# Hyena's transforms ahead of retention's six projections in the program's order

## The chip, the core and the metric

The kernel runs on one core of a Trainium2 chip. The core's engines run side by side, each through its own list of instructions in the order of that list, and they wait for each other at semaphores: TensorE (PE, with its weight loads as PEld), VectorE (DVE), ScalarE (ACT), GpSimd (POOL) and SyncE (SP), which here only issues DMAs. The metric is the device time of one execution in microseconds (us), lower is better.

## The reference

One inference step of a two-layer trunk over 384 token rows: 128 context tokens and 256 latent tokens, model width 1024. Each layer does, with norms and modulation vectors that come from a condition vector:

```
h = rms_norm(x) * (1 + scale1) + shift1
ret, hy, gqa, mla = split(h @ w_in)
y = concat(retention(ret), hyena(hy), attention(gqa), latent_attention(mla)) @ w_out
x = x + gate1 * rms_norm(y)
h = rms_norm(x) * (1 + scale2) + shift2
x = x + gate2 * rms_norm((silu(dwconv3(h @ up_gate)) * (h @ up_val)) @ w_down)
```

The mixers that matter here are two. Hyena takes three slices of 256 channels, convolves them over three neighbours, and then does, for two orders in turn, a long convolution by way of a Fourier transform:

```
z = x1 * ifft(fft(v) * spec0)
y_hy = x2 * ifft(fft(z) * spec1)
```

Retention projects queries, keys and gates, forms decayed scores q.k over 4 heads, sums them with the values and a carried state, normalises by head and multiplies by silu(gate). The context group also returns its retention state.

## The kernel before

All matrix products of the model's width are done in a split form: a weight unit of 512 KB is loaded by a DMA into a tile `raw` (a ring of five, `wraw`, L361), ACT casts it to `whi` (L358), DVE takes the rest as `wlo` (L359), each in two halves, and PE multiplies three times (`mm3`, L382 to L385). One input projection of 128 channels (`fm_mm`, tile `fmps`) is 24 matmuls of 386 columns. The pairs `whi`, `wlo` of the mixers form a ring of three.

In each layer the mixers come in the program's order latent attention, grouped attention (`gqa`), Hyena, retention, output projection. Attention up to its last key projection stands in an order written out by hand; from there to the output projection a scheduler places instructions. It walks through time on a model of the engines, takes on each engine what is ready, and among several the one that stands first in the program. So the program's order is a priority, and what stands behind can fill gaps. Once built, the order on each engine is fixed, and so is the order of the DMAs on SP's queue.

Hyena and retention are generators, each cut in two by a `yield`:

- `hyena` (L1069): the first part is six projections, the short convolution (L1078 to L1080) and transposes to token rows (`hyt`, L1095). The second part is the transforms: for each of two orders, six forward matmuls (`hyR`, `hyI`, `hyQ`, L1102 to L1105), a product with the spectrum `spec` on DVE (`Y`, with a scratch tile `t12`, L1113 to L1117) whose last sum is POOL's (L1118), and the inverse: `hyAB`, `hyP` (L1122 to L1126) and the multiplication by x1 (`hz`, `ut`, L1130 to L1136) in the first order, `hyF` (L1142 to L1146) and the multiplication by x2 in the second.
- `retention` (L1160): the first part is value tables and the six projections (L1180 to L1189), the second is decays, scores (`rpc`, `rsc`), sums (`rob`), norms (`rrb`, L1267) and the result.

A third strand is the modulation vectors. Layer 0 has to compute those of two groups of its own (`Ada`): 16 steps, each of which loads two 512 KB tiles `araw` through the same ring of five and multiplies them (`adaps`, L407). A step is taken from the list `side` by each projection (`fm_proj`) and by each of Hyena's two orders (L1100); `run(side[0])` does what is left. In layer 1 the list has one short step.

`spec` has one buffer. Layer 1's spectrum is loaded into it by a DMA of 1536 KB that is written in the feed-forward part of layer 0 (L1548) and may go once layer 0's Hyena has read the old one for the last time.

Behind the mixers stands the output projection (`acc`, L1283 to L1285), with eight weight units, and its first matmuls are the filler for retention's second part.

Of the kernel before, what the change touches and what calls it, by code (L numbers as in the profile page):

```python
# [268 lines left out]
def trunk(ctx: ExitStack, tc: tile.TileContext, A, O, offs, depth=DEPTH):  # L269
# [79 lines left out]
    def bank(tag="a", name="bk"):  # L349
        kw = {"bufs": 1} if tag == "n" else {}  # L350
        return (pa if tag == "a" else pm).tile([128, 512], F32, tag=tag, name=name, **kw)
# [9 lines left out]
    def wraw(src, n=1024):  # L361
        raw = wr.tile([128, 1024], F32, tag="raw", name="raw")[:, 0:n]
        nc.sync.dma_start(out=raw, in_=src)
        return raw

    def wparts(n=1024, pool=None, bufs=4):
        kw = {"bufs": bufs} if pool is not None else {}
        return [(pool or wh).tile([128, 1024], F32R, tag=g, name="w" + g, **kw)[:, 0:n] for g in ("hi", "lo")]

    def wsplit(raw, hi, lo, h, eng=None):  # L370
        n = raw.shape[1] // 2
        sl = slice(h * n, h * n + n)
        split(raw[:, sl], hi[:, sl], lo[:, sl], eng)
# [89 lines left out]
    def ada(a, out, k1=8, part=False):  # L463

        for k in range(a.k0, k1):
            a.load(k)
            a.mm(k, last=k1 - 1)
            if k < k1 - 1:
                yield
        if part:  # L470
            a.hold(k1)
        else:
            a.load_end()
            a.end()
            a.columns()
            a.vec(out)
        yield

    def ada_last(a, out):
        a.columns()  # L480
        a.vec(out)
        yield
# [41 lines left out]
    def gate_tiles(ggp):  # L524
        return [ggp.tile([128, D], F32, tag="gg", name="gg", bufs=2) for _ in range(2)]
# [5 lines left out]
    def load_lp(l):  # L531
        t = lpp.tile([128, A["lp"].shape[2]], F32, tag="lp", name="lp")
        nc.sync.dma_start(out=t, in_=A["lp"][l])

        def get(name, a=0, b=None):
            o, w = poff[name]
            return t[:, o + a:o + (w if b is None else b)]

        fh = lpp.tile([128, NF, 4], F32, tag="ffh", name="ffh")
        V.tensor_scalar(fh.rearrange("p f t -> p (f t)"), get("ffc"), 0.5, None, ALU.mult)  # L540

        lg = get("lg")
        W = lg.shape[1]
        e = sm.tile([128, W], F32, tag="lge", name="lge", bufs=1)
        s = sm.tile([128, W], F32, tag="lgs", name="lgs", bufs=1)
        s2 = sm.tile([128, W], F32, tag="lgs2", name="lgs2", bufs=1)
        pol = sm.tile([128, W], F32, tag="lgp", name="lgp", bufs=1)
        lgt = lpp.tile([128, W], F32, tag="lgt", name="lgt")
        S.activation(out=e, in_=lg, func=ACTF.Abs)
        S.activation(out=e, in_=e, func=ACTF.Exp, scale=-1.0)  # L550
        V.tensor_scalar(s, e, 2.0, None, ALU.add)
        V.reciprocal(s, s)
        V.tensor_tensor(out=s, in0=e, in1=s, op=ALU.mult)
        V.tensor_tensor(out=s2, in0=s, in1=s, op=ALU.mult)
        V.tensor_scalar(pol, s2, 2.0 / 19, 2.0 / 17, ALU.mult, ALU.add)
        for d in (15, 13, 11, 9, 7, 5, 3, 1):
            V.tensor_tensor(out=pol, in0=pol, in1=s2, op=ALU.mult)
            V.tensor_scalar(pol, pol, 2.0 / d, None, ALU.add)
        V.tensor_tensor(out=pol, in0=pol, in1=s, op=ALU.mult)
        V.scalar_tensor_tensor(out=lgt, in0=lg, scalar=0.0, in1=pol, op0=ALU.min, op1=ALU.subtract)  # L560
        return get, fh, lgt
# [148 lines left out]
    def retention_tables(lgt, pool, **kw):  # L710
        lag = pool.tile([128, 384], F32, name="lag", **kw)
        nc.sync.dma_start(out=lag, in_=A["lag"])
        return rettab(lgt, lambda: pool.tile([128, 384], F32, name="tabt", **kw), lag)
# [111 lines left out]
    def run(g):  # L825
        for _ in g:
            pass
# [538 lines left out]
    for l in range(depth):  # L1366
# [4 lines left out]
        with ExitStack() as ph:  # L1371
            mt = ph.enter_context(tc.tile_pool(name="mt", reuse_waits="tile", bufs=1))
            lmt = mt.tile([128, A["lm"].shape[2]], F32, tag="lm", name="lm")

            def M(name):
                o, w = moff[name]
                return lmt[:, o:o + w]

            mx = ph.enter_context(tc.tile_pool(name="mx", reuse_waits="tile", bufs=1))
            myc = tc.tile_pool(name="my", reuse_waits="tile", bufs=1, side="right")  # L1380
            my = myc.__enter__()

            jobs = [ada_last(ahead.pop((l, 1)), vecs)] if l else [ada(Ada(l, 1), vecs), ada(Ada(l, 2), vecs)]
            side[:] = [(s for j in jobs for s in j), 0]
            tma = mx.tile([128, 3, 416], F32, tag="tma", name="tma")
            tmb = my.tile([128, 3, 384], F32, tag="tmb", name="tmb")
            wa, wb = pj, TokProj(l, "wtb", 384, ht)
            us = []
            ml = mla(l, mx, my, M, tmb, tma, wb.acc)
            gq = gqa(l, mx, my, M, hi, lo, tma, lambda: get("sink"), us)  # L1390
            with tc.manual_schedule(engines=CORE | {mybir.EngineType.SP}):
                wa.raw(3)
                for c in range(4):
                    wb.raw(c)
                wa.cut(3, 0)
                wa.cut(3, 1)
                wa.part(3, (0, 1, 2))
                uw = [wraw(A["win"][l, 2])]
                nc.sync.dma_start(out=lmt, in_=A["lm"][l])
                next(ml)  # L1400
                next(gq)
                if l == 0:
                    nc.sync.dma_start(out=cst, in_=A["cst"])
                wb.cut(0, 0)
                wb.cut(0, 1)
                wa.out(tma)
                wb.part(0, (0, 1, 2))
                uw.append(wraw(A["win"][l, 0]))
                for c in range(1, 4):
                    wb.cut(c, 0)  # L1410
                    wb.cut(c, 1)
                    wb.part(c, (0, 1, 2))
                next(ml)
                us.append(wparts())
                wsplit(uw[0], *us[0], 0)
                wsplit(uw[0], *us[0], 1)
                next(ml)
                next(gq)
                us.append(wparts())
                wsplit(uw[1], *us[0], 0)  # L1420
                wsplit(uw[1], *us[0], 1)
                next(ml)
                next(gq)
                end = V.tensor_copy(zero8, zero8)
            if l == 0:
                mkf = hm.tile([128, 256], F32, tag="hm", name="mkf")
                nc.sync.dma_start(out=mkf, in_=A["mask"])
                with tc.issue_after(end.ins):
                    V.tensor_copy(maskb, mkf)
                    lps = load_lp(0)  # L1430
                    rt = retention_tables(lps[2], mx, tag="w15", bufs=11)
            get, fh, lgt = lps
            run(ml)
            run(gq)
            hyg = hyena(l, mx, my, get, sp, hi, lo)
            reg = retention(l, mx, M, get, rt, hi, lo, tma)
            next(hyg)
            next(reg)
            run(side[0])
            run(hyg)  # L1440
            side[0] = iter(())
            myc.__exit__(None, None, None)
            run(reg)

            wqc = tc.tile_pool(name="wq", reuse_waits="tile", bufs=4, side="right")
            wq = wqc.__enter__()
            gg = gate_tiles(wq)

            b6 = [bank("m" if i < 5 else "n", "acc") for i in range(6)]
            acc = [b6[0:2], [b6[2], b6[5]], b6[3:5]]  # L1450
            with tc.manual_schedule(engines={mybir.EngineType.SP}):
                early = [(wunit(A["wout"][l, k]), mixout[k]) for k in (6, 7, 4)]
                for ts in ((0, 1), (2,)):
                    for j, e in enumerate(early):
                        down_step(acc, *e, T0, j == 0, False, ts)
                ws = [(wunit(A["wout"][l, k]), mixout[k]) for k in (5, 2, 3)]
                ws += [(wunit(A["wout"][l, k], 1024, wq), mixout[k]) for k in (0, 1)]
                up_w = [wunit(A["wup"][l, u], 1024, wq) for u in (0, NF)]
                for r in range(2):
                    gate_load(gg, 2 * (l % 2), r)  # L1460
# [158 lines left out]
```

## Time and profile before

| what | us |
|---|---|
| median of 3 runs | 1088.33 (1086.99 to 1088.36) |
| the profiled execution | 1084.69 |
| its span, first to last instruction | 1082.9 |
| PE busy | 1059.6 (98%) |
| DVE busy | 727.2 (67%) |
| ACT busy | 504.3 (47%) |
| POOL busy | 61.5 (6%) |

PE's busy time includes the run of a matmul through the array, so a full PE row does not mean that each instruction followed the one before at once; the distance from start to start tells that. In layer 0 Hyena's and retention's work of interest lies from 165 to 238 us, in layer 1 from 690 to 758 us.

### The profile page before, as it was taken

To read this page: it belongs to the slowest core of one execution; us is meant where nothing else is said; L and a number is where in the kernel's file an instruction comes from. 1 tells how busy PE (TensorE), PEld (TensorE's weight loads), DVE (VectorE), ACT (ScalarE), POOL (GpSimd) and SP (SyncE) were. 2 spreads that over 40 slices of the span, in tenths; PEclk is the share of its full clock that TensorE was granted. 3 is DMA by queue.
4 is the path that set the end of the run, shared out by engine and by line. 5 is a ranking of instruction groups with operands and counts; after the bars stand their busy time and mean duration, and the time that the engine had idled before them with its cause. 6 is when DMAs were issued, how large, how long until landed. Compare 5 with 4: busy or idle time off the path is not lost.

```text
span 1082.9 us, 15620 instructions
## 1 busy us (share of the span) xinstructions
PE 1059.6 (98%) x5763; PEld 894.1 (83%) x5763; DVE 727.2 (67%) x1544; ACT 504.3 (47%) x1106; POOL 61.5 (6%) x74
## 2 busy tenths in 40 slices
PE   9999999999889999999999999999999999999997
PEld 4496767768789999899996977886899999999996
DVE  5868965476789885799557577757766455545544
ACT  5754635334734344333447454552584344334333
POOL 2210000000200000000002000001020000000000
PEclk9999999999999999999999999999999999999999
DMA  9674345855576764577356522231535433443301
GB/s 345 231 278 169 118 155 178 302 168 222 180 250 201 226 215 150 159 234 221 124 169 209 179 79 77 60 97 41 217 109 191 129 117 118 136 131 122 119 19 58
DMA packets 53017, 176.05 MB, mean 163 GB/s; under 512 B 8618, under 2 KB 10538, under 8 KB 52429
## 3 DMA queue, kind: packets, MB, share of 16 engines
q1 hardware_dynamic: 49229, 171.19, 47.2%
q10 hardware_dynamic: 3712, 3.87, 1.0%
q8 instruction: 45, 0.74, 0.3%
q14 instruction: 31, 0.25, 0.1%
HBM read 169.60 MB, written 5.44 MB: 162 GB/s over the span
## 4 chain that ended last, share of the span: by engine, by line
PE 86%; DVE 8%; DMA 2%; ACT 2%; issue 1%; POOL 0%; ACTq 0%; DVEq 0%; SPq 0%; POOLq 0%
PE ups L383 5%; PE ups L385 5%; PE ups L384 5%; PE gps L383 5%; PE facc L1283 5%; PE facc L1285 5%; PE gps L385 5%; PE gps L384 5%; PE facc L1284 5%; PE fmps L383 4%; PE fmps L385 4%; PE fmps L384 4%; PE adaps L407 2%; PE acc L1283 2%; PE acc L1284 2%; PE acc L1285 2%
## 5 line engine op out<-in xcount | busy, mean ns | idle before, releaser
L359 DVE TENSOR_TENSOR wlo<-raw,whi 128x512 fp32r<-128x512 f32 (+2 forms) x388 | 254.4, 686 | 169.0 <-ACT whi L358 168.5
L358 ACT CAST whi<-raw 128x512 fp32r<-128x512 f32 (+2 forms) x388 | 221.6, 611 | 276.5 <-DMA raw<-in_wdn_dram 99.1
L1283 PE MATMUL facc<-whi,fah 128*128 128x512 f32 x264 | 105.3, 399 | 2.7 <-ACT fah L358 2.7
L1285 PE MATMUL facc<-whi,fal 128*128 128x512 f32 x264 | 104.5, 397 | 0.2 <-DVE fal L359 0.2
L1284 PE MATMUL facc<-wlo,fah 128*128 128x512 f32 x264 | 104.5, 396 | 0.0
L505 DVE SCALAR_TENSOR_TENSOR avc<-avr,cs,avc 128x1024 f32<-128x1024 f32 x56 | 70.3, 1282 | 0.3 <-DMA avr<-in_ada_dram 0.2
L383 PE MATMUL gps<-hTa,whi 128*128 128x386 f32 (+4 forms) x184 | 62.5, 340 | 0.0
L383 PE MATMUL ups<-hTb,whi 128*128 128x386 f32 (+4 forms) x184 | 61.7, 335 | 0.6 <-ACT hTb L812 0.6
L384 PE MATMUL ups<-hTb,whi 128*128 128x386 f32 (+4 forms) x184 | 61.4, 334 | 0.8 <-POOL hTb L815 0.8
L385 PE MATMUL gps<-hTa,wlo 128*128 128x386 f32 (+4 forms) x184 | 62.0, 337 | 0.0
L384 PE MATMUL gps<-hTa,whi 128*128 128x386 f32 (+4 forms) x184 | 61.8, 336 | 0.0
L383 PE MATMUL gps<-hTb,whi 128*128 128x386 f32 (+4 forms) x184 | 61.7, 335 | 0.0
L383 PE MATMUL ups<-hTa,whi 128*128 128x386 f32 (+4 forms) x184 | 61.7, 335 | 0.0
L385 PE MATMUL ups<-hTb,wlo 128*128 128x386 f32 (+4 forms) x184 | 61.5, 334 | 0.0
L385 PE MATMUL gps<-hTb,wlo 128*128 128x386 f32 (+4 forms) x184 | 61.4, 334 | 0.0
L385 PE MATMUL ups<-hTa,wlo 128*128 128x386 f32 (+4 forms) x184 | 61.4, 334 | 0.0
L384 PE MATMUL ups<-hTa,whi 128*128 128x386 f32 (+4 forms) x184 | 61.3, 333 | 0.0
L384 PE MATMUL gps<-hTb,whi 128*128 128x386 f32 (+4 forms) x184 | 61.3, 333 | 0.0
L1285 PEld LDWEIGHTS facc<-whi,fal 128*128 128x128 f32 x264 | 50.0, 189 | 13.1 <-DVE fal L359 1.3
L1283 PEld LDWEIGHTS facc<-whi,fah 128*128 128x128 f32 x264 | 50.0, 189 | 13.0 <-ACT fah L358 3.0
L1284 PEld LDWEIGHTS facc<-wlo,fah 128*128 128x128 f32 x264 | 50.0, 190 | 10.1
L1299 ACT ACTIVATE fth<-fc 128x386 f32<-128x386 f32 x44 | 23.2, 528 | 59.9 <-DVE fc L1298 59.9
(381 smaller groups left out, 2371.4 us busy)
## 6 DMA issues: line engine op xcount, KB each, us to landing
raw<-in_wup_dram SPq DMA_DIRECT2D x88, 512.0 KB
araw<-in_ada_dram SPq DMA_DIRECT2D x64, 512.0 KB
raw<-in_wdn_dram SPq DMA_DIRECT2D x44, 512.0 KB
avr<-in_ada_dram SPq DMA_DIRECT2D x32, 512.0 KB
raw<-in_win_dram SPq DMA_DIRECT2D x30, 512.0 KB
raw<-in_wout_dram SPq DMA_DIRECT2D x16, 512.0 KB
gg<-gd SPq DMA_DIRECT2D x8, 512.0 KB
raw<-in_wta_dram SPq DMA_DIRECT2D x8, 416.0 KB
```

Of the source, the lines that this page charges most:

```text
L358: S.copy(hi, src)
L359: (eng or V).tensor_tensor(out=lo, in0=src, in1=hi, op=ALU.subtract)
L383: T.matmul(out, ah, bh, start=start, stop=False)
L384: T.matmul(out, ah, bl, start=False, stop=False)
L385: T.matmul(out, al, bh, start=False, stop=stop)
L407: T.matmul(self.ps[32 * j:32 * j + 32, :], cs[:, k, :], rows[j // 2][:, 512 * (j % 2):512 * (j % 2) + 512], start=(k == self.k0), stop=(k ...
L505: V.scalar_tensor_tensor(out=acc[:, v, c], in0=raw, scalar=sc, in1=acc[:, v, c], op0=ALU.mult, op1=ALU.add)
L1283: T.matmul(acc[t][h], ah[:, cs_], wh_[:, hs], start=first, stop=False)
L1284: T.matmul(acc[t][h], ah[:, cs_], wl_[:, hs], start=False, stop=False)
L1285: T.matmul(acc[t][h], al[:, cs_], wh_[:, hs], start=False, stop=last)
L1299: S.activation(out=th, in_=c, func=ACTF.Tanh)
```

## The change

```
@@ -1434,10 +1434,10 @@
             run(gq)
             hyg = hyena(l, mx, my, get, sp, hi, lo)
             reg = retention(l, mx, M, get, rt, hi, lo, tma)
-            next(hyg)
+
+            run(hyg)
             next(reg)
             run(side[0])
-            run(hyg)
             side[0] = iter(())
             myc.__exit__(None, None, None)
             run(reg)
```

Before, the program had Hyena's projections, retention's projections, Hyena's transforms, retention's second part. Now it has Hyena's projections, Hyena's transforms, retention's projections, retention's second part. No instruction of the model's arithmetic is added or taken away. In layer 0, the two steps of the list `side` that Hyena's orders ask for now find something to take, so two steps of the modulation vectors move ahead of retention's first projection.

PE in layer 1, before: from the second half of the first order's forward matmuls on.

```order
L1104 MATMUL hyQ<-ut,cst 128x256
L1105 MATMUL hyQ<-ut,cst 128x256
L1204 MATMUL rkt<-cst_79,rf_7091 128x128
L1204 MATMUL rkt<-cst_79,rf_7126 128x128
L1283 MATMUL acc<-whi,mix 128x512
L1284 MATMUL acc<-wlo,mix 128x512
L1285 MATMUL acc<-whi,mix 128x512
L1213 MATMUL rst<-rpack 64x128 x4
L1225 MATMUL rpc<-rf_7021,rf_7091 128x128
L1225 MATMUL rpc<-rf_7056,rf_7126 128x128
L1283 MATMUL acc<-whi,mix 128x512
L1122 MATMUL hyAB<-Y,cst 128x256 x2
```

The same place of layer 1 in the changed kernel, up to the second order's first matmul (`rf` are retention's projected rows, `mix` the mixers' results).

```order
L1104 MATMUL hyQ<-ut,cst 128x256
L1105 MATMUL hyQ<-ut,cst 128x256
L1122 MATMUL hyAB<-Y,cst 128x256 x2
L1124 MATMUL hyAB<-Y,cst 128x256 x2
L1125 MATMUL hyP<-Y,cst 128x256
L1126 MATMUL hyP<-Y,cst 128x256
L1102 MATMUL hyR<-ut,cst 128x256
```

And the end of the second order there, where the projections follow.

```order
L1105 MATMUL hyQ<-ut,cst 128x256
L1142 MATMUL hyF<-cst,Y 128x128 x4
L1144 MATMUL hyF<-cst,Y 128x128 x4
L1145 MATMUL hyF<-cst,Y 128x128 x2
L1146 MATMUL hyF<-cst,Y 128x128 x2
L383 MATMUL fmps<-hTa,whi 128x386
```

Retention's tail no longer stands between Hyena's matmuls; from the first `hyt` to the last `hyF` of layer 1 PE's list has nothing but Hyena, and four of retention's six projections (96 matmuls) follow in one piece. The other two stand ahead of `hyt`, as fillers of grouped attention, before and now.

SP's queue in layer 0, before: from Hyena's last weight unit (`raw_1853`) to retention's second (`raw_1979`); the first is `raw_1927`.

```order
L363 DMA raw_1853<-in_win_dram 128x1024
L399 DMA araw_1900<-in_ada_dram 128x1024
L399 DMA araw_1902<-in_ada_dram 128x1024
L422 DMA abg_1908<-in_adag_dram 128x1024
L363 DMA raw_1927<-in_win_dram 128x1024
L399 DMA araw_1962<-in_ada_dram 128x1024
L399 DMA araw_1964<-in_ada_dram 128x1024
L399 DMA araw_1971<-in_ada_dram 128x1024
L399 DMA araw_1973<-in_ada_dram 128x1024
L363 DMA raw_1979<-in_win_dram 128x1024
```

The same stretch of SP's queue in the changed kernel, up to retention's first weight unit, now `raw_2048`.

```order
L363 DMA raw_1853<-in_win_dram 128x1024
L399 DMA araw_1890<-in_ada_dram 128x1024
L399 DMA araw_1892<-in_ada_dram 128x1024
L422 DMA abg_1898<-in_adag_dram 128x1024
L399 DMA araw_1959<-in_ada_dram 128x1024
L399 DMA araw_1961<-in_ada_dram 128x1024
L399 DMA araw_2040<-in_ada_dram 128x1024
L399 DMA araw_2042<-in_ada_dram 128x1024
L363 DMA raw_2048<-in_win_dram 128x1024
```

Four loads of modulation weights stand ahead of retention's first unit that stood behind it; the unit takes the place that its second unit had, and on PE the first of retention's projections moves from ahead of grouped attention's last softmax to behind eight `adaps` matmuls that follow it.

A second place on the same queue in the changed kernel: layer 1's spectrum, between retention's third unit (`raw_2142`) and its fourth (`raw_2193`).

```order
L363 DMA raw_2142<-in_win_dram 128x1024
L399 DMA araw_2177<-in_ada_dram 128x1024
L399 DMA araw_2179<-in_ada_dram 128x1024
L1548 DMA spec_3535<-sd_96 128x3072
L399 DMA araw_2185<-in_ada_dram 128x1024
L399 DMA araw_2187<-in_ada_dram 128x1024
L363 DMA raw_2193<-in_win_dram 128x1024
```

Before, this DMA stood behind all of retention's units and behind seven of the eight of the output projection.

## Rows read from the trace of the kernel before

**Rows 1.** The page's first part: busy us, share, instructions.

```profile
PE 1059.6 (98%) x5763; PEld 894.1 (83%) x5763; DVE 727.2 (67%) x1544; ACT 504.3 (47%) x1106; POOL 61.5 (6%) x74
```

**Rows 2.** Waits of PE, whole span: us in total, times, longest us.

```profile
PE tps L799 <- DVE xn L792: 4.5, 3, 2.0
PE hyF L1144 <- POOL Y L1118: 1.1, 2, 0.7
```

**Rows 3.** Windows of layer 1: busy PE, PEld, DVE, ACT, POOL, clock, DMA, GB/s.

```profile
730.00:740.00 10.00, 10.00 (x51) 6.83 (x51) 8.62 (x22) 0.74 (x2) 1.99 (x2) 1.00 0.08 13
740.00:750.00 10.00, 9.57 (x68) 6.00 (x69) 8.63 (x25) 1.43 (x4) 2.72 (x4) 1.00 0.18 55
```

**Rows 4.** Timeline of PE, layer 1: start, us, instruction, [idle before].

```profile
722.06 0.34 PE L383 MATMUL fmps<-hTa,whi 128*128 128x386 f32 x1
...
726.32 0.59 PE L1102 MATMUL hyR<-ut,cst 128*128 128x256 f32 x2
...
727.18 0.59 PE L1102 MATMUL hyR<-ut,cst 128*128 128x256 f32 x2
...
737.33 0.59 PE L1102 MATMUL hyR<-ut,cst 128*128 128x256 f32 x2
...
743.45 1.16 PE L1144 MATMUL hyF<-cst,Y 128*128 128x128 f32 x8 [0.43 <-POOL Y L1118]
```

**Rows 5.** Timeline of DVE, layer 1.

```profile
708.17 1.23 DVE L1091 COPY fo<-cv 128x128 f32<-128x128 f32 x2
...
728.33 0.69 DVE L1113 TENSOR_TENSOR Y<-hyR,spec 128x512 f32<-128x512 f32 x1
...
732.79 0.43 DVE L1114 TENSOR_TENSOR t<-hyQ,spec 128x256 f32<-128x256 f32 x1 [0.72 <-POOL Y L1118]
...
736.35 0.42 DVE L1135 TENSOR_TENSOR ut<-hz 128x256 f32<-128x256 f32 x1
...
737.02 1.41 DVE L1242 TENSOR_TENSOR rW<-rsc,tab 128x256 f32<-128x256 f32 x4
738.89 0.69 DVE L1113 TENSOR_TENSOR Y<-hyR,spec 128x512 f32<-128x512 f32 x1 [0.46 <-PE hyR L1102]
```

**Rows 6.** Timeline of POOL, layer 1.

```profile
731.49 1.27 POOL L1118 TENSOR_TENSOR Y<-Y,t 128x512 f32<-128x512 f32 x1 [22.18 <-DVE t L1117]
...
744.93 0.72 POOL L1118 TENSOR_TENSOR Y<-Y,t 128x256 f32<-128x256 f32 x1 [1.54 <-DVE t L1117]
```

**Rows 7.** Timeline of PE, layer 0, end of grouped attention.

```profile
169.06 0.45 PE L383 MATMUL fmps<-hTa,whi 128*128 128x386 f32 x1
...
171.29 0.82 PE L925 MATMUL ptp<-cst,P 128*128 128x128 f32 x6
...
178.64 1.92 PE L407 MATMUL adaps<-araw,cs 128*32 128x512 f32 x16
```

**Rows 8.** Timeline of DVE, layer 0, the last long softmax.

```profile
170.48 1.40 DVE L922 TENSOR_SCALAR P<-P,rc 128x384 f32<-128x384 f32 x4
```

**Rows 9.** Timeline of SP's queue, layer 0: start of issue, us, DMA.

```profile
156.58 0.33 SPq L363 DMA_DIRECT2D raw<-in_win_dram  x1
...
173.53 0.33 SPq L363 DMA_DIRECT2D raw<-in_win_dram  x1
...
227.39 0.33 SPq L1548 DMA_DIRECT2D spec<-sd  x1
```

**Rows 10.** Windows of both layers, columns as in Rows 3.

```profile
792.00:793.00 1.00, 0.00 (x0) 0.00 (x0) 0.96 (x2) 0.83 (x3) 0.91 (x1) 1.00 0.00 0
794.00:797.00 3.00, 3.00 (x16) 3.00 (x15) 1.37 (x4) 1.56 (x5) 0.72 (x2) 0.50 0.02 5
620.00:625.00 5.00, 3.57 (x11) 1.74 (x10) 3.90 (x7) 4.63 (x11) 0.00 (x0) 1.00 0.45 132
210.00:215.00 5.00, 4.90 (x28) 4.14 (x27) 3.71 (x12) 2.15 (x5) 0.73 (x1) 1.00 0.88 313
```

**Rows 11.** DMA issues, whole span: what, count, KB each.

```profile
spec<-sd SPq DMA_DIRECT2D x1, 1536.0 KB
```

More of the change, by code (lines that the diff above doesn't have):

```diff
@@ L1436, in trunk @@
             reg = retention(l, mx, M, get, rt, hi, lo, tma)
-            next(hyg)
+            run(hyg)
             next(reg)
             run(side[0])
-            run(hyg)
             side[0] = iter(())
```

## The prediction

> **What bounds the kernel now.** I read the page's first part, then PE's waits, then windows and timelines of the two stretches in which Hyena and retention lie. PE is busy for 1059.6 of 1082.9 us [rows 1]; there is no second engine near it, and anything that leaves PE without work is added to the time. The waits of PE are few: the longest group, 4.5 us, lies at norms outside the stretches that the change touches, and of Hyena's transforms 1.1 us are on record, for POOL's sum ahead of `hyF` [rows 2]. The reader is to see in the windows of layer 1 that PE is full, or nearly, from 730 to 750 us while DVE works 8.6 of 10 us [rows 3]: two chains, Hyena's transforms and retention's tail, alternate there, and each fills PE while the other waits for DVE. That cover is what the change takes away. So there is next to nothing to win: 0.4 us of idle in layer 1 [rows 3, 4], the other 0.7 us of the `hyF` wait in layer 0, and perhaps 0.6 us where PE changes less often between the transforms and the 512-column matmuls of the output projection.
>
> **Layer 1: the transforms alone on PE.** In the changed order PE has nothing but Hyena from `hyt` to the last `hyF`. I work out how long that chain is by itself, and how much of it is PE's own work.
>
> The chain, first order. From `hyR` to DVE's first product: 737.33 to 738.89, that is 1.56 us [rows 4, 5]. From that product to the new `ut` that the second order needs: 728.33 to 736.35 plus its 0.42 and a hand-over of 0.1, 8.5 us, of which one product of retention (0.33 us) was in DVE's way and goes: 8.2 us [rows 5]. In it lies the wait of DVE for POOL, which holds the only scratch tile for 1.27 us [rows 5, 6]; that stays, since POOL's sums are the same. Sum 9.8 us. Second order: again 1.56 us, then from the product at 738.89 to the end of POOL's second sum at 744.93 + 0.72 [rows 5, 6], 6.8 us, then the last two `hyF`, some 0.6 us: 9.0 us. Both: 18.8 us.
>
> PE's own work in it: 18 matmuls of 256 columns, of which `hyR` and `hyI` take 0.86 us together (726.32 to 727.18), 0.43 us each, 7.7 us; 12 of 128 columns, of which four take 1.1 us (743.45), 0.27 us each, 3.2 us; and some ten restarts at an estimated 0.1 us. That is 11.9 us [rows 4]. So PE stands 18.8 - 11.9 = **6.9 us**. Bounds: 5 us if the hand-overs that I read beside other work are shorter by themselves, 8.5 us if each of some eight hand-overs costs 0.2 us more than in my reading.
>
> Two smaller terms. Ahead of `hyR` the transposes wait for copies of DVE that take 1.23 us from 708.17 [rows 5], beside POOL's products of retention; before, two projection matmuls stood in that wait and now none: **0.5 us** (0 to 1). And retention's tail now has only the output projection between its parts. PE there waits for DVE's four products `rW` (1.41 us at 737.02 [rows 5]) before each of the two sums `rob`, which Hyena's matmuls covered; 0.3 us of `rob` on other inputs and what there is of the output projection take some of it off: 1 us for each, **2.0 us** (1 to 3). Four projections in one piece take 4 x 4.26 us (722.06 to 726.32 for one [rows 4]), as before; their weights have long landed. Less the 0.4 us and the 0.6 us named above, layer 1 costs 0.5 + 6.9 + 2.0 - 1.0 = **8.4 us**.
>
> **Layer 0: the weights come later.** Here the transforms do have fillers: nine to eleven projection matmuls and a few `adaps` in each gap. Going through the same chain with them between, I find gaps of 0.8 us in all (0 to 4, the upper end if the fillers' weights are late): **0.8 us**. The costs come from SP's queue.
>
> First, retention's first unit is issued behind four more loads of modulation weights. It waits for a ring buffer that comes free late, as its second unit did before: at 173.53 instead of 156.58 [rows 9]. Its 24 matmuls, 4.3 us of PE, began at 169.06 and ran inside grouped attention's last softmax [rows 7]. Without them PE stands from 169.06 until the first normalised scores, which DVE begins at 170.48 [rows 8]: 1.85 us; and 0.9 us more in the waits between `ptp` at 171.29 and the scores before 178.64, where five of the 24 stood. The rest of the 24 covered nothing and is merely done later. **2.8 us** (1.5 to 4.3, all of it).
>
> Second, layer 1's spectrum. Its DMA was issued at 227.39 [rows 9], behind all of retention's weights; now it stands ahead of retention's fourth unit and blocks the queue until Hyena's last read of the old spectrum. Layer 0's first `hyR` I put near 185.5: the eight `adaps` of 178.64 [rows 7] start 1.4 us earlier without projections ahead of them and end at 179.2, and 14 projection matmuls (2.5 us), the short softmax and `hyt` (3.8 us, an estimate) follow. The last read is about 19 us behind it, by the chain above with fillers in its gaps: 204.7. Then 1536 KB of spectrum, two `araw` and the unit itself, 512 KB each, must come in [rows 11], 3 MB in all, at the 313 GB/s that the stretch from 210 to 215 us showed [rows 10]: 10 us, so the unit lands near 214.5, and cast and remainder take 1 us more. PE has 1.8 us of `adaps` behind the chain's end near 206.5, one projection (4.3 us) and 1 us of `adaps`, and is there at 213.6. **2.0 us** for this unit, **0.7 us** for the next one, which queues behind it (together 0 to 6: nothing if the chain is through earlier or the spectrum shares the DMA engines gently, 6 if the unit lands last of all that is queued). DVE and ACT are not in the way there: they wait for the same weights. Third, retention's tail as in layer 1, with a little more filler: **1.5 us** (0.5 to 3). Less 0.7 us of old waits, layer 0 costs 2.8 + 0.8 + 2.7 + 1.5 - 0.7 = **7.1 us**.
>
> **The sum.** 8.4 + 7.1 = 15.5 us. The profiled execution took 1084.69 us with a span of 1082.9, so its changed counterpart would take 1100.2. The three timed runs have their median 3.64 us above the profiled execution, at 1088.33, and the forecast goes by them: 1103.8, **1104 us**. Behind the mixers everything is bound to PE's own order, so nothing absorbs the delay; the feed-forward parts are moved as a whole.
>
> **Rivals.**
> *PE's clock falls in the new gaps.* In layer 1's norms PE's longest wait is 2.0 us [rows 2]; from 792 to 793 it had nothing at all, with the granted clock still at 1.00, and from 794 to 797 it worked all the while with the clock at 0.50, its lower level of 1.2 GHz [rows 10]. Three us at half speed cost 1.5 us. Against it: from 620 to 625 PE was busy only 3.57 of 5 us, in shorter pauses, and the clock stayed at 1.00 [rows 10]. The new gaps of layer 1 are 0.6 to 1.5 us each by the chain above, seven in a row; the one at 169.06 in layer 0 is 1.85 us. If four of them bring a fall, it is 6 us more, 1110 us.
> [...]
>
> *Only layer 1 pays.* If layer 0's weights are in time after all, because PE, held up, also asks later, and the grouped attention finds its cover in `adaps`, layer 0 costs nothing: 1088.3 + 8.4 = 1097 us. For it: PE was busy for 4.90 of 5 us where the DMA engines were fullest before [rows 10], so weights were in time. Against it: the missing 24 matmuls at 169.06 are in the order, whatever lands when.
>
> *The two chains gain by being apart* (the other side). DVE is at 8.6 of 10 us where they run together [rows 3]. If that made each of them slow, so that PE's full row there hides weight loads and drains rather than work, then retention's tail by itself, with a free DVE and Hyena's results long there for the output projection, would run through it without a wait, and the transforms would cost only the difference. It decides from the point at which retention's tails are shorter than before by more than all the terms above, 15.5 + 1.7 us in two layers. If the tail by itself took as much off as the transforms add, and 1.7 us of old waits were won beside, the time would be 1088.3 - 1.7 = 1087 us. I see no row for it beyond DVE's share; the idle on record leaves it only those 1.7 us and what PE's restarts hide.
>
> **How the numbers follow.** The forecast has 0.60, the clock 0.20, layer 1 alone 0.15, the gain 0.05. The terms' own bounds make 5 to 11 us of layer 1 and 1.5 to 13 of layer 0, not all at one end at once. For 8 in 10 I take 1095 to 1113 us: it holds the forecast's middle, layer 1 alone, and most of the clock's case. 0.2%, some 2 us, is what a measurement of this kernel can tell from none. Slower by more than that is all of the first three cases, 0.94 with a remnant of the fourth taken off; the fourth is split between no change, 0.04, and faster, 0.02.
>
> **What would show it.** In layer 1, PE's timeline between the first `hyR` and the first projection behind the last `hyF` should be about 19 us long, with idle of 6 to 7 us put down to DVE's `Y`, POOL's `Y` and ACT's `hbs`; PE's wait list should have `hyAB`, `hyP`, `hyR` and `hyF` in it, where now only `hyF` is. Retention's `rob` should wait for `rW`. In layer 0, PE should stand for near 2 us ahead of `ptp` at about 169 us, and a projection should wait for ACT's `whi` or DVE's `wlo` at about 214 us, with the spectrum's DMA issued near 205. The forecast is wrong if PE is as full in 726 to 750 us as before, or if the gaps are there and the out-projection behind them has become shorter by as much.

## The result, and the profile after

The changed kernel took 1103.64 us (median of 4 runs, 1100.11 to 1108.62) against 1087.66 us for the kernel before in the runs beside it: a ratio of 1.0155, 95% interval 1.0111 to 1.0199. It is slower, and the forecast of 1104 us holds to 0.4 us. A second set of runs of the same kernel gave 1106.45 us and 1.0186 (1.0167 to 1.0206). What follows shows that the total was met with sizes and causes that were partly others than those of the working.

The profiled execution took 1103.06 us, with a span of 1101.3. The page's first part answers to [rows 1]:

```profile
PE 1067.1 (97%) x5763; PEld 895.4 (81%) x5763; DVE 729.1 (66%) x1544; ACT 504.5 (46%) x1106; POOL 62.6 (6%) x74
```

PE has the same 5763 instructions and stands 34.2 us instead of 23.3. But it is also 7.5 us longer *busy* with them. So a list of waits tells only part of the loss.

PE's waits over the whole span, as in [rows 2] (us in total, times, longest):

```profile
PE ptp L925 <- DVE P L922: 2.7, 2, 1.9
...
PE fmps L383 <- ACT rf L1182: 1.4, 1, 1.4
PE hyAB L1122 <- DVE Y L1115: 1.4, 1, 1.4
PE hyF L1144 <- POOL Y L1118: 1.2, 2, 0.8
...
PE hyR L1102 <- DVE ut L1135: 0.9, 1, 0.9
...
PE fmps L383 <- ACT whi L358: 0.9, 1, 0.9
PE hyAB L1124 <- POOL Y L1118: 0.8, 1, 0.8
...
PE fmps L385 <- DVE wlo L359: 0.8, 1, 0.8
...
PE hyP L1126 <- POOL Y L1118: 0.4, 1, 0.4
PE rob L1260 <- ACT rsq L1258: 0.4, 1, 0.4
```

The waits that were named are there, but for one: `ptp` in layer 0's softmax, the four kinds at Hyena's transforms in layer 1 (for DVE and POOL, none for ACT's `hbs`), `whi` and `wlo` in layer 0. Retention's `rob` does not wait for `rW`, but 0.4 us for ACT's `rsq`. One was not named: 1.4 us ahead of a projection, for ACT's copy `rf`.

Where the time lies is read stage by stage. The rows of the transposes `tps` mark each norm in PE's timeline; the table has the time from the start of the last such row in one norm to that in the next, in us, for all kernels of this study. "Rest" runs from layer 1's second norm to PE's last matmul:

| profiled run | layer 0 mixers | layer 0 feed-forward | layer 1 mixers | rest | falls of PE's clock to 0.50 within the mixers, near | timed ratio to before |
|---|---|---|---|---|---|---|
| before | 233.5 | 301.3 | 206.4 | 281.9 | none | 1 |
| after | 242.8 | 298.5 | 217.5 | 281.9 | 728 | 1.0155 |
| e0_after_again | 244.1 | 298.8 | 218.9 | 282.3 | 165, 698, 726 | 1.0186 |
| e1_l1_only | 233.6 | 300.6 | 217.9 | 281.9 | 731 | 1.0097 |
| e2_l0_only | 242.5 | 299.2 | 206.4 | 285.0 | none | 1.0075 |
| e3_after_whole | 238.1 | 298.6 | 216.3 | 281.4 | none | 1.0127 |
| e4_before_whole | 232.9 | 300.3 | 206.3 | 280.7 | none | 0.9997 |
| e5_after_spec_pool | 247.9 | 298.3 | 216.4 | 281.2 | 172, 220 | 1.0211 |
| e6_after_scratch | 242.6 | 300.1 | 215.5 | 285.1 | 172 | 1.0186 |
| e7_after_hzf | 244.2 | 299.2 | 208.7 | 284.8 | 174 | 1.0127 |
| e10_after_noside | 242.3 | 298.9 | 217.8 | 284.8 | 228, 727 | 1.0181 |
| e11_after_speclate | 242.7 | 300.5 | 216.6 | 280.7 | 174 | 1.0171 |
| e12_after_all | 237.5 | 298.6 | 210.5 | 283.4 | 754 | 1.0052 |
| e13_mix | 240.4 | 300.9 | 206.4 | 283.4 | 164, 226 | 1.0042 |

(Some expectations below count from the last single transpose, which gives 0.5 to 0.7 us more a layer and the same differences.) The change costs 9.3 us in layer 0 and 11.1 in layer 1 (10 in e3, e5 and e11, whose clock did not fall there), and the profiled run of after is 2.7 us shorter in layer 0's feed-forward. The column "rest" has its own fall: in the runs with 284.8 us and more (e2, e6, e7, e10) the clock stays at 0.50 for some 10 us behind layer 1's second norm.

**Layer 1.** PE's timeline from the first `hyR` to the first projection behind the last `hyF`, which answers to [rows 4] (start, us, instruction, idle before it):

```profile
716.29 0.70 PE L1102 MATMUL hyR<-ut,cst 128*128 128x256 f32 x2
...
720.52 1.10 PE L1122 MATMUL hyAB<-Y,cst 128*128 128x256 f32 x4 [1.37 <-DVE Y L1115]
722.43 1.13 PE L1124 MATMUL hyAB<-Y,cst 128*128 128x256 f32 x4 [0.81 <-POOL Y L1118]
...
724.69 0.70 PE L1126 MATMUL hyP<-Y,cst 128*128 128x256 f32 x2 [0.38 <-POOL Y L1118]
726.33 0.67 PE L1102 MATMUL hyR<-ut,cst 128*128 128x256 f32 x2 [0.94 <-DVE ut L1135]
...
727.64 1.06 PE L1102 MATMUL hyR<-ut,cst 128*128 128x256 f32 x2
728.50 1.06 PE L1103 MATMUL hyI<-ut,cst 128*128 128x256 f32 x2
...
731.63 1.13 PE L1142 MATMUL hyF<-cst,Y 128*128 128x128 f32 x8 [0.78 <-DVE Y L1115]
733.54 1.16 PE L1144 MATMUL hyF<-cst,Y 128*128 128x128 f32 x8 [0.78 <-POOL Y L1118]
...
735.79 0.71 PE L1146 MATMUL hyF<-cst,Y 128*128 128x128 f32 x4 [0.42 <-POOL Y L1118]
737.93 0.44 PE L383 MATMUL fmps<-hTa,whi 128*128 128x386 f32 x1 [1.42 <-ACT rf L1182]
```

The reader is to see three things. The transforms are alone, 20.2 us long, with 5.5 us of idle. From the `hyR` at 727.64 to the row behind it there are 0.86 us, where the first order took 0.43. And the first projection waits another 1.42 us. The windows of that stretch (columns as in [rows 3]):

```profile
724.00:726.00 2.00, 1.01 (x4) 0.30 (x2) 1.96 (x5) 0.00 (x0) 0.63 (x1) 1.00 0.00 0
726.00:728.00 2.00, 1.67 (x5) 1.45 (x6) 0.52 (x2) 0.00 (x0) 0.00 (x0) 0.72 0.00 0
728.00:730.00 2.00, 2.00 (x6) 1.57 (x5) 1.10 (x2) 0.00 (x0) 0.00 (x0) 0.50 0.00 0
```

The granted clock is at 0.50, 1.2 GHz, from about 727 to 730, behind two in which PE was busy half of the time. By PE's starts, Hyena's matmuls take 3.1 us longer than before without their waits; in e3_after_whole, whose clock did not fall there, 1.4. So the fall costs 1.7 us (0.7 of it taken off the waits) and the restarts of the bare chain 1.4. Retention's tail takes 1.6 us more, in this run and in e3 and e7 alike. With 6.6 us more idle (5.5 in the transforms, 1.4 ahead of the projection, 0.4 at `rob`, less 0.7 of old waits) this is 11.3 us of the 11.1.

ACT's timeline shows where the 1.42 us come from:

```profile
723.60 0.37 ACT L1128 COPY hbs<-hyAB 128x256 f32<-128x256 f32 x1 [6.57 <-PE hyAB L1124]
736.32 0.27 ACT L1148 COPY hbs<-hyF 128x128 f32<-128x128 f32 x1 [12.35 <-PE hyF L1146]
737.22 0.27 ACT L1148 COPY hbs<-hyF 128x128 f32<-128x128 f32 x1 [0.63 <-DVE hd L1151]
737.38 0.88 ACT L1182 ACTIVATE rf<-fmps 128x386 f32<-128x386 f32 x2
```

Retention's first two projections are done by 714.2 us. ACT has nothing to do from 724 to 736, and copies them out only at 737.38, behind `hyF`'s copies. Until then both PSUM buffers of the projections are held. e7 below takes this up.

**Layer 0.** PE's timeline, which answers to [rows 7], and SyncE's queue, which answers to [rows 9]. PE first:

```profile
156.14 1.07 PE L407 MATMUL adaps<-araw,cs 128*32 128x512 f32 x8
157.13 0.45 PE L383 MATMUL fmps<-hTa,whi 128*128 128x386 f32 x1
...
171.69 0.85 PE L925 MATMUL ptp<-cst,P 128*128 128x128 f32 x6 [1.91 <-DVE P L922]
...
191.53 1.05 PE L407 MATMUL adaps<-araw,cs 128*32 128x512 f32 x4
192.51 1.13 PE L1124 MATMUL hyAB<-Y,cst 128*128 128x256 f32 x4
193.58 1.05 PE L407 MATMUL adaps<-araw,cs 128*32 128x512 f32 x4
...
218.44 0.45 PE L383 MATMUL fmps<-hTa,whi 128*128 128x386 f32 x1 [0.91 <-ACT whi L358]
```

The queue (start of issue, us until the last of the row is issued, DMA):

```profile
157.23 13.38 SPq L399 DMA_DIRECT2D araw<-in_ada_dram  x4
174.28 0.33 SPq L363 DMA_DIRECT2D raw<-in_win_dram  x1
...
206.82 0.33 SPq L1548 DMA_DIRECT2D spec<-sd  x1
207.42 2.88 SPq L399 DMA_DIRECT2D araw<-in_ada_dram  x2
210.39 0.39 SPq L363 DMA_DIRECT2D raw<-in_win_dram  x1
```

Retention's first unit is issued at 174.28 behind four `araw`, the spectrum at 206.82, and PE stands 1.91 us ahead of `ptp` at 171.69, all as forecast. What no list of waits shows is in the rows of `adaps`. One step of the modulation vectors is four matmuls into four strips of 32 rows, eight in the trace's records. Eight records in one piece take 0.99 us from start to start (156.14 to 157.13), and four take 0.98 (191.53 to 192.51), with `hyAB` between them and the other four. So a step that is parted costs 0.98 us for each piece, and PE counts as busy. Over layer 0 the same 160 records took 23.2 us before and 27.6 after: three steps were parted by the order, and a fourth by an `araw` that came in late. That is 4.4 us; the waits are 4.5 us more (`ptp` and `pv` 2.3, weights 1.7, `acc` 0.4), and 0.4 lie in the rest.

**Layer 0's feed-forward.** The window near 306 us in the kernel before:

```profile
304.00:309.00 5.00, 2.91 (x7) 2.33 (x8) 5.00 (x11) 2.61 (x5) 0.00 (x0) 0.67 0.55 178
```

The same place in after, 9 us later:

```profile
313.00:318.00 5.00, 2.84 (x13) 2.06 (x13) 5.00 (x10) 2.61 (x5) 0.00 (x0) 1.00 0.57 201
```

Before's clock fell here, behind a wait of 2.7 us for `fah`; after has that wait too, 2.2 us long, and its clock stayed up. This gives most of the 2.7 us back. It is no property of the change alone: the three profiles with the old order in layer 0 have a fall near 306 us, but three of the eleven with the new order (e6, e11, e13) have one near 315.

### The profile page after: what moved, and what is told of

Read it like the earlier page. It is cut to its first block, busy times and chain, and to the rows that moved or that the text cites. A ratio compares the mean times of both kernels' runs of the same rounds, so it can differ in the third digit from the quotient of the medians.

```text
span 1101.3 us, 15630 instructions
## 1 busy us (share of the span) xinstructions
PE 1067.1 (97%) x5763; PEld 895.4 (81%) x5763; DVE 729.1 (66%) x1544; ACT 504.5 (46%) x1106; POOL 62.6 (6%) x74
## 4 chain that ended last, share of the span: by engine, by line
PE 87%; DVE 7%; ACT 2%; DMA 2%; issue 1%; POOL 1%; ACTq 0%; DVEq 0%; SPq 0%; POOLq 0%
PE gps L383 5%; PE ups L383 5%; PE ups L385 5%; PE gps L385 5%; PE ups L384 5%; PE gps L384 5%; PE facc L1283 5%; PE facc L1285 5%; PE facc L1284 5%; PE fmps L383 3%; PE fmps L385 3%; PE fmps L384 3%; PE adaps L407 2%; PE acc L1284 2%; PE acc L1285 2%; PE acc L1283 2%
## 5 line engine op out<-in xcount | busy, mean ns | idle before, releaser
L1285 PEld LDWEIGHTS facc<-whi,fal 128*128 128x128 f32 x264 | 49.6, 188 | 11.9
L1299 ACT ACTIVATE fth<-fc 128x386 f32<-128x386 f32 x44 | 23.3, 529 | 57.1 <-DVE fc L1298 57.1
```

What stands on the lines that cost most here:

```text
L1285: T.matmul(acc[t][h], al[:, cs_], wh_[:, hs], start=False, stop=last)
L1299: S.activation(out=th, in_=c, func=ACTF.Tanh)
```

## The experiments

**e1 and e2: one layer at a time** (edit shortened).

```
-            run(hyg); next(reg); run(side[0])
+            if l == 1:                      # e2: if l == 0
+                run(hyg); next(reg); run(side[0])
+            else:
+                next(hyg); next(reg); run(side[0]); run(hyg)
```

> The new order in layer 1 alone; layer 0 stands as before. The traces of before and after put layer 1 (from its first norm's last transpose to its second norm's) at 207.1 and 218.1 us, 11.0 more. Theory (the terms of the two layers are independent, and 11.0 is the change's own cost): 1087.7 + 11.0 = 1098.7 us, with the pauses at hyAB, hyP, hyR and hyF and the 1.4 us ahead of the third retention projection as in after. If the half-speed stretch at 726.5 to 730.5 us was a chance of that one execution, some 2 us less: 1096.5. Rival (layer 1 is late only because it inherits layer 0's delays): within 1 us of 1087.7.

> The new order in layer 0 alone; layer 1 stands as before. Theory: layer 0 costs 9.3 us by the two traces (its part up to the second norm's last transpose took 234.0 us before and 243.3 after), and the 2.7 us that the feed-forward of layer 0 was shorter in after are a clock dip of before's one profiled execution: 1097.0 us. If these 2.7 us belong to the change (Hyena done earlier lets later weights come earlier): 1094.3. Rival (only layer 1 pays): 1088 or less.

e1: 1.0097 (1.0070 to 1.0124), 10.5 us; e2: 1.0075 (1.0057 to 1.0093), 8.1 us. Together 18.6 us, against 16.9 and 20.2 in the two sets of runs of after: the layers are independent, and the rivals by which only one pays are out. In the table each has its own layer's cost and not the other's.

**e3 and e4: `adaps` steps in one piece**, in the changed kernel and in the one before (edit shortened).

```
-            for j in range(4):
-                T.matmul(self.ps[32 * j:32 * j + 32, :], ...)
+            for j in (2, 3, 0, 1):          # the later half's DMA first
+                # 2nd to 4th: high priority, each ordered behind the last
+                m = T.matmul(self.ps[32 * j:32 * j + 32, :], ...)
```

> The changed kernel, but the four adaps matmuls of one step, which write four strips of 32 rows of a PSUM bank, are issued in one piece instead of being parted by other work. In after's trace any piece of a step takes 0.98 us, whether it has one of the four matmuls or all; 7 pieces too many by the order, 3 of them in Hyena's stretch of layer 0. Theory (a piece costs its full 0.93 to 0.98 us of PE wherever it stands): 1103.6 - 6.7 = 1097 us, with adaps rows in steps of 0.98 for whole steps only. Rival (in Hyena's pauses the pieces fill time that PE would stand anyway): the 3 there give nothing, 1103.6 - 3.8 = 1100. Second rival (DVE's chain sets the pace in all these stretches, in latent attention too): 1103.6, no change.

> The kernel before, with the four adaps matmuls of a step in one piece. By its order and trace 4 pieces too many go, all in latent and grouped attention (83 to 151 us). Theory (a piece costs PE its 0.93 to 0.98 us, and PE is full there): 1087.7 - 3.8 = 1083.9 us. Rival (they fill gaps): 1087.7.

e4: 0.9997 (0.9978 to 1.0017), no change, as its rival said. `adaps` took 3.9 us less of PE and the first `hyt` came 3.3 us earlier behind the norm, but 2.7 of these went again behind it. e3: 1.0127 (1.0112 to 1.0143), 1099.9 us, which is the first rival's time; layer 0 takes 238.1 us instead of 242.8. Its gain lies ahead of the first `hyt`, 4.9 us; from the first `hyR` to the last `hyF` it is 1.1, and behind them 1.4 are lost, since PE waits for `araw` there:

```profile
211.74 1.06 PE L409 MATMUL adaps<-araw,cs 128*32 128x512 f32 x8 [0.91 <-DMA araw<-in_ada_dram]
```

The pieces too many ahead of `hyt`, from 83 to 151 us, stand in the kernel before as well, so e3's 4.9 us are for the most part no cost of the change. What the change costs with whole steps is read from e3 against e4: 5.2 us in layer 0 (238.1 less 232.9) instead of 9.3, nearly all of it waits (11.0 us of idle against 6.2). By this, 4.1 of the 9.3 us hang on parted steps. That the pieces among Hyena's transforms alone make them is not shown: from the first `hyt` on, e3 is no shorter than after, because without the pieces PE waits for loads instead.

**e0: the changed kernel again.**

> The changed kernel once more, unaltered, beside the variants of this call. Theory: 1.0155 times before, some 1102 to 1104 us; layer 1 (last transpose of its first norm to the last of its second) 217.5 us, layer 0 242.8, layer 0's feed-forward 298.5. If the half-speed stretch at the second hyR of layer 1 comes from the pauses ahead of it, it is there again, and layer 1 takes 217 to 218; if it was a chance, layer 1 takes 216.

The ratio was 1.0186, and each layer took 1.3 to 1.4 us more than expected. The clock fell in the transforms again, but earlier, in the first order, and near 165 and 698 us as well:

```profile
724.44 2.07 PE L1124 MATMUL hyAB<-Y,cst 128*128 128x256 f32 x4 [0.80 <-POOL Y L1118]
726.30 1.06 PE L1125 MATMUL hyP<-Y,cst 128*128 128x256 f32 x2
```

In e3 the same chain, with its waits of up to 1.45 us, kept the full clock. Of the eight profiled runs with bare transforms in layer 1, four have a fall there or just behind (after, e0, e1, e10) and four have none (e3, e5, e6, e11). So falls come in the new gaps in some executions and not in others.

**e5 and e11: the spectrum's DMA**, from GpSimd's queue, and behind retention's last weight unit (edit shortened: `wlast` is the DMA of that unit).

```
-                        nc.sync.dma_start(out=sp, in_=sd[l + 1])
+                        nc.gpsimd.dma_start(out=sp, in_=sd[l + 1])      # e5
+                        with tc.issue_after(wlast):                     # e11
+                            nc.sync.dma_start(out=sp, in_=sd[l + 1])
```

> The changed kernel with layer 1's spectrum loaded through GpSimd's queue instead of SyncE's; nothing else. Theory (the spectrum's DMA blocks the queue ahead of retention's fourth weight unit): the waits for araw, whi and wlo at 216.3 to 219.2 us, 0.22 + 0.91 + 0.26 us on record, and the 1 us that an adaps step lost there by its parted arrival go, 2.2 us in all: layer 0 takes 240.6 instead of 242.8 us, the kernel 1101.4 us. Rival (the spectrum's 1536 KB take the same DMA engines at the same time, whichever queue issues them): layer 0 stays within 0.5 us of 242.8.

> The changed kernel with layer 1's spectrum loaded behind retention's last weight unit in SyncE's queue; nothing else. When GpSimd's queue issued it, it started at the same 207 us, and layer 0 became 4 to 5 us longer, with 3.0 us of waiting for araw: so not the blocked queue but the 1536 KB on the DMA engines, ahead of the weights, would be what costs. Theory by that: with the spectrum behind the weights, the waits for araw, whi and wlo between 215 and 219.5 us go, and the parted adaps step with them, 2 to 2.4 us: layer 0 takes 241 us against 242.8 and 244.1, the kernel 1101.5 to 1104. Rival (the loads that are queued there are late without the spectrum too, because SyncE's queue stands for ring buffers): layer 0 within 0.7 us of 242.8 to 244.1.

e5's layer 0 is 3.8 us longer than e0's, which had a fall ahead of `hyt` too, and the ratio 1.0211 (1.0183 to 1.0240): theory and rival both fell. The spectrum was issued at 207.53, where after has 206.82; now PE waited longer for `araw`, with a fall of the clock behind that. Why the other queue made it worse is not settled. PE's wait in e5:

```profile
PE adaps L407 <- DMA araw<-in_ada_dram: 3.0, 1, 3.0
```

e11's ratio, 1.0171 (1.0144 to 1.0199), is not apart from e0's. Its layer 0, 242.7 us, has to be set beside e0's 244.1 and e7's 244.2, which had a fall in the same stretch: it costs 1.6 us from the last long scores to the first `hyt` (21.2 us in all three, 19.6 in after and e2). So 1.4 us are won; from the last `hyF` to `rkt` e11 takes 24.1 us, the others 25.6 to 25.9. The theory held for two thirds of its size. SyncE's queue in e11:

```profile
197.85 13.62 SPq L401 DMA_DIRECT2D araw<-in_ada_dram  x4
211.56 0.38 SPq L365 DMA_DIRECT2D raw<-in_win_dram  x1
...
219.79 0.42 SPq L1552 DMA_DIRECT2D spec<-sd  x1
```

Retention's fourth unit is not issued earlier: 1.8 us behind the start of the last `hyF` row, as in after (210.39 and 208.58). The `araw` ahead of it stand in the queue until then with or without the spectrum. What costs is the spectrum's 1536 KB among the loads, not its place in the queue: from 215 to 220 us the share of the DMA engines is 1.02 in after and 0.88 in e11.

**e6: no wait of DVE for POOL's scratch tile** (edit shortened).

```
-                t12 = my.tile([128, 2, 2, 256], F32, tag="mv", name="t12")
+                t12 = my.tile([128, 2, nb, 256], F32, tag="mv" if nb == 2 else "ckvT", name="t12")
```

> The changed kernel with a scratch tile of its own for the last third of each of Hyena's products (a buffer that is free at that time), so that DVE no longer waits 1.1 us in each order for POOL's sum to give the only scratch tile back. Theory (in layer 1 the transforms run alone, and this wait is on their chain): layer 1 is 2.2 to 3 us shorter, 217.5 to about 215; layer 0, where other work fills, stays within 0.5 us: kernel 1101. Rival (PE and POOL set the pace there): no change in layer 1.

Layer 1 took 215.5 us, against 216.3 to 216.6 in e3, e5 and e11: 1 us of the 2.2 to 3 expected. Part of it came back as a wait of 1.8 us at `hyR` for `ut`, where there were 0.9. Layer 0, where nothing was expected, won 1.5 us against e0 and e7; its transforms took 20.6 instead of 22.5 us. The ratio, 1.0186 (1.0164 to 1.0208), does not show it.

**e7: `hzf` in another ring of buffers.**

```
-                    z = mx.tile([128, 384], F32, tag="w15", name="hzf", bufs=11)
+                    z = mx.tile([128, 384], F32, tag="PT", name="hzf", bufs=3)
```

> The changed kernel with Hyena's two results hzf in another buffer ring (tag PT, 3 buffers, instead of w15, 11 buffers), nothing else. In after's trace ACT copies retention's first two projections out of PSUM (rf) only behind hyF's copies, and PE waits 1.4 us for that ahead of the third projection. Theory (rf takes its buffer from the same ring behind hzf, since the ring is handed out in the program's order; until then both PSUM banks of the projections are held, and so no projection can stand in Hyena's pauses): with its own ring for hzf 38 projection matmuls, 6.8 us of PE's work, stand between layer 1's transforms, and layer 1 takes 217.5 - 8.5 = 209 us, the kernel 1095 us. What stays is retention's tail, some 2 us, and layer 0. Rival (program order alone parts the two chains, and the fillers only lengthen Hyena's chain): layer 1 216 us or more, the kernel 1102 or more. In layer 0 nothing should change.

Layer 1 took 208.7 us, 8.8 less than after and 10.2 less than e0, as the theory said. The kernel, 1.0127 (1.0107 to 1.0147), came out at 1100.2 us, 6.2 less than e0 beside it and not the 1095 expected; in its profile layer 0 has a fall of the clock (1.6 us) that after has not, and the rest is 2.9 us longer. The window of e7's transforms in layer 1, columns as in [rows 3]:

```profile
719.00:739.00 20.00, 18.72 (x100) 16.08 (x101) 15.13 (x30) 4.50 (x10) 4.05 (x5) 1.00 0.16 52
```

Two rows of PE's timeline in it:

```profile
723.54 1.05 PE L1122 MATMUL hyAB<-Y,cst 128*128 128x256 f32 x4
725.35 1.13 PE L1124 MATMUL hyAB<-Y,cst 128*128 128x256 f32 x4 [0.41 <-POOL Y L1118]
```

PE is busy 18.7 of 20 us with projections between the transforms, the clock stays up, and `hyAB` waits 0.41 us where it waited 1.37 and 0.81. ACT's timeline in e7 has `rf` ahead of `hyF`'s copies:

```profile
717.24 0.50 ACT L1182 ACTIVATE rf<-fmps 128x386 f32<-128x386 f32 x1
...
730.10 0.49 ACT L1182 ACTIVATE rf<-fmps 128x386 f32<-128x386 f32 x1
...
738.89 0.27 ACT L1148 COPY hbs<-hyF 128x128 f32<-128x128 f32 x1 [7.80 <-PE hyF L1146]
```

So it is not enough that retention's projections come later in the program: in the same order, e7 fills the transforms with them. The transforms of layer 1 were bare because `rf` and `hzf` draw on one ring, and after the change `hzf` stands ahead of `rf` in it.

**e10: no modulation steps among the transforms.**

```
         for o in range(2):
-            next(side[0], None)
```

> The changed kernel without the two places in Hyena's transforms that run a step of the modulation vectors ahead; these steps then come behind retention's projections in the program, so that retention's first weight unit is loaded before them, and fewer adaps and no parted ones by them stand among the transforms of layer 0. Theory (the 2.3 us more that PE waits in grouped attention's last long softmax, 169 to 173 us, come from that unit being late): the waits at ptp and pv go back to 0.8 us; the second order of Hyena has less filler and costs 1 to 2 us, so that layer 0 takes 240 to 242 us against 242.8 and 244.1, the kernel 1101 to 1104. Rival (the unit would not have helped, since DVE sets the pace in the softmax): ptp waits 2.7 us as in after.

Retention's first unit is issued at 156.79 again, and the softmax's wait is gone; others stand in its place (e10's waits of PE):

```profile
PE fmps L383 <- ACT rf L1181: 2.4, 2, 1.4
...
PE adat L446 <- DVE sb L437: 2.1, 1, 2.1
...
PE fmps L383 <- ACT whi L358: 1.4, 1, 1.4
...
PE ptp L925 <- DVE P L922: 0.8, 1, 0.8
```

Layer 0 takes 242.3 us (240 to 242 expected), the kernel 1.0181 (1.0156 to 1.0206). The 2.3 us did come from the late unit. Most of them were lost again at `adat`, for which PE waits 2.1 us near 226 with a fall of the clock behind it.

**e12 and e13: all four edits together; and with them layer 0 new, layer 1 old.** Their edits are those of e3, e7, e10 and e11.

> The changed order with four of its costs taken out together: hzf in a ring of its own, adaps steps in one piece, no modulation steps among the transforms, the spectrum behind retention's last weight unit. Theory (the costs are those of the runs alone, and they add): layer 1 takes 208.7 us as with hzf's own ring; layer 0 243 less 2.3 (softmax), 2 (spectrum) and 4 (pieces) = 235; layer 0's feed-forward 298.5 to 299: the kernel 1103.6 - 8.8 - 8 = 1087 us, no more than 0.3% from before. What stays against before is retention's tail with little beside it, 2 us a layer. Rival (in layer 0 the DMA engines are the bound, and each mended cost shows up as another wait): layer 0 240 us, the kernel 1092.

> Layer 0 as in the kernel with all four costs taken out, layer 1 in the order of before (and its hzf in the old ring). Theory: layer 1 206.4 us as before, layer 0 235, its feed-forward 298.5 to 299 instead of 300.5 to 301, since in the five profiles with the new order in layer 0 PE's clock did not fall near 304 us, and in the three with the old order it did: 1087 - 2.3 = 1085 us, 0.1 to 0.3% less than before. Rival (the fall near 304 us comes and goes by chance; layer 0 costs more): 1088 or more.

e12: 1.0052 (1.0030 to 1.0073), layer 0 237.5 us, halfway between theory and rival, layer 1 210.5 with a fall near 754. By its time, 1091.3 us, e12 is at the rival's 1092. e13: 1.0042 (1.0020 to 1.0064), 1088.3 us, within its rival's "1088 or more"; the fall that the theory took to be gone from layer 0's feed-forward is there, near 315. Two thirds of the loss are won back; no order that was run beats the one before. What the last 4 us of layer 0 are is not settled: in e12 PE waits there 2.3 us for `sb` ahead of `adat` and 1.7 us for `whi`.

## Why the prediction came out, point by point

- **Transforms alone in layer 1: 6.9 us.** e3, at full clock, has 19.2 us (711.62 to 730.82) with 6.2 of waits; after itself 20.2 and 5.5. Against the 11.9 us that I gave to PE's own work (before has 11.9 too, by its starts) e3's chain is 7.3 us longer, so the step held in size. Its reason was too thin: I read from the order that nothing fills, and did not ask what keeps the projections from filling (e7: the ring).
- **The wait for `rf`, 1.4 us,** was missed, for the same reason: "their weights have long landed" is right, but a projection also needs a PSUM buffer. The 0.5 us at the transposes did not come (no wait at `hyt` in after), and no run shows the 0.6 us that I took off for fewer changes of shape: in layer 1 Hyena's and retention's matmuls ran slower than before, not faster.
- **Retention's tail, 2.0 us:** 1.6 us of slower running and 0.4 at `rob` in layer 1; 2.3 us are left in e7 against before. Held in size; it shows as restarts rather than as waits for `rW`. In layer 0 the 1.5 us did not come: retention's tail there has no wait and takes 0.7 us less by its starts.
- **PE's clock** was a rival with 0.20 and came in part: one fall in layer 1 for a net 1.2 us (after against e3), where the rival had four for 6. The Trainium skill tells in "TensorE: Matmul & The Clock Gate", section "HAM oscillation — how this bites in real kernels", of a kernel whose clock is throttled again at each of its waits for DMA, which it puts at some 3 to 5 us. The gaps among layer 1's transforms are shorter, none of them over 1.9 us; after, e0 and e10 had a fall there all the same, and e3, e5, e6 and e11 had none. So the trace agrees in part, and the measurement decides.
- **Lost cover in the softmax, 2.8 us:** 2.3 measured, and e10 shows the cause as stated.
- **The spectrum, 2.7 us:** waits of 1.7 us more came, near 218 instead of 214 and, for the next unit, near 226, and e11 gives 1.4 to the spectrum. I had its DMA hold up the queue; it does not (e5, e11: the `araw` behind it are issued no earlier without it), it only takes its share of the transfers.
- **Gaps of layer 0's transforms, 0.8 us:** right as waits (`hyF` 0.8 against 0.7 before), wrong as a cost. This is the step that failed: I counted fillers as work moved, not as work that can grow. Parted `adaps` steps made PE busy for 4.4 us more, and by e3 against e4 4.1 of layer 0's 9.3 us hang on them; how much of that PE would have waited for loads instead stays open. The 0.7 us of old waits that I took off in layer 0 stayed as well.
- **The sum:** 8.4 + 7.1 forecast, 11.1 + 9.3 measured, less 2.7 in the feed-forward and 0.7 more ahead of the mixers: 18.4 us from span to span against 15.5. By the medians it is 16.0. That the total fits so closely is luck. What was missed or put too low (the clock, `rf`, the parted steps) was offset in part by terms that did not come. The profiled run of before, from which the terms were read, had a fall of the clock in layer 0's feed-forward that after did not have, and the median of before came out 0.7 us lower this time. The second set of runs of the same kernel, 20.0 us above before, would not have fitted so well.

## What to carry to other kernels

Before two parts of a program are parted, look at what they share: a ring of buffers that is handed out in program order can keep work from filling gaps that its place in the order allows. Count busy time as well as waits: the matmuls that run side by side in strips cost 0.98 us here for each piece that the scheduler cut them into. And a cost that is taken out alone, in a stretch with several late loads behind it, comes back in large part as the next wait (e4, e10); four at once won two thirds of the loss.

## What the runs showed of the hardware

Within the mixers the granted clock falls to 0.50 for some 3 us at a time, behind gaps, and not in every execution at the same gap: second `hyR` in after and e10, second `hyAB` in e0, nothing in e3; the softmax's 1.9 us gap was followed by a fall in e5, e6, e7 and e11 and by none in after, e0 and e2. One such fall costs 1.2 to 1.7 us. That is as much as the single edits here are worth, and the runs of one kernel spread by 1.4 to 11 us. Stage times of profiles, compared where the falls are the same, told edits apart that the ratios could not; each rests on one execution.
